# A two-layer decoder on one core: more pairs by seven products, the last norm by token halves, and one constant on another queue

## The chip, the cores and the metric

The kernel runs on one core of one Trainium2 chip. The metric is the device time of one execution in microseconds (us); the median of three runs is given. TensorE (PE; PEld is its weight load), VectorE (DVE), ScalarE (ACT) and the DMA queues of SyncE (SP) and ACT do the work; GpSimd (POOL) only sets up constants.

## What is computed

The reference is a trunk of two layers on 256 tokens of width 2048, in float32. Layer 0 mixes tokens by a causal pooling mixer, layer 1 by differential attention (8 heads, two softmax maps each, subtracted); after each comes a SwiGLU block with inner width 5632; RMS norm ahead of every part and at the end.

```python
for i in range(2):
    hn = rmsnorm(h, norm_mix[i])
    mix = pool_mixer(hn, ...) if i == 0 else diff_attention(hn, ...)
    h = h + mix
    hn = rmsnorm(h, norm_ffn[i])
    h = h + (silu(hn @ w_gate[i]) * (hn @ w_up[i])) @ w_down[i]
return rmsnorm(h, final_norm)
# diff_attention: q, k, v = hn @ w_qkv; a = softmax(q1 k1) - lam * softmax(q2 k2) with ALiBi;
# o = rmsnorm(a @ v, subln_g) * (1 - lambda_init); return o @ w_o
```

## The kernel before

All weight matrices are streamed once, in pieces of 1 MB: a *pair* is 256 rows (two blocks of 128) by 1024 columns (two blocks of 512). `load` brings it (three buffers `raw`, SP's queue), and `halves` splits it into a rounded part `whi` (ACT, line 118) and the remainder `wlo` (DVE, line 119), both in fp32r, since a product in fp32r carries too few bits for one to be enough: each product is made as hi x hi, hi x lo, lo x hi, three TensorE instructions of 128x512 (line 180). The activations (`xp`, `xq`, `h`, `oT`) are held as hi and lo, too, transposed.

`group` makes one product of 256 tokens by 1024 columns over all pairs of a group, in eight PSUM banks `b0` to `b7`. A pair is either *plain*, 8 block products (24 instructions) into the four banks of the result (b4 to b7), or *by seven*, a Strassen-Winograd product: 7 block products (21 instructions) into all of b0 to b6. A pair by seven needs sums of the weight's blocks on DVE (`sums`, lines 124, 126, 127) and their split into `thi` (ACT, 133) and `tlo` (DVE, 134), with one buffer each of tsum, thi and tlo, and an activation operand in eight blocks (`pair` with `seven`, lines 249 to 257, through the buffer `e`) instead of four. Products over different pairs are added up in the banks, so which pairs go by seven is free for each group; the tuples `SEVEN`, `SEVEN_DOWN`, `SEVEN_QK` list them. If a group has a pair by seven, `combined` adds the banks up (two ACT copies, eight DVE operations, lines 190 to 200); if it has none, the banks are the result themselves. Transposes and small products use b0 to b3 (`aux`), too.

The order is: pool mixer (lines 266 to 346), SwiGLU of layer 0 (`ffn`), q and k of four groups of heads, v and attention's output by heads, w_o, SwiGLU of layer 1. In `ffn` the 11 gate/up groups come in chunks of 4, 4 and 3; behind each chunk come two down groups (o = 0, 1), whose pairs are the h tiles of the chunk, 8, 8 and 6. In the first gate/up group of each layer only pair 6 goes by seven, in the others 2, 4 and 6. Down has pairs 2 and 5 by seven, but none in the last group of layer 1. After the last chunk the residual's square sums are made (`square_sum`, line 220), and either the next operand is transposed or, at the end, the row scale is computed for all tokens (`row_scale`), and four `ys` tiles of 512 columns are scaled and stored (lines 402 to 412).

The Tile framework reorders the instructions of each engine when the kernel is built, by priorities and its own cost model; each engine then runs its list in order. So the order in the code is not always that of the trace.

The start: x (2 MB in four DMAs) goes on SP's queue, `band` (the pooling matrices, 768 KB) and the gains on ACT's; two plain pool weights follow on SP, and `scale_in` (1 MB) and `dist` on ACT. Per token half the squares of x give a row scale, band is multiplied by it (line 296), and only then come TensorE's first products (lines 313 to 315).

Of the kernel before, what the change touches and what calls it, by code (L numbers as in the profile page):

```python
# [9 lines left out]
F32 = mybir.dt.float32  # L10
F32R = mybir.dt.float32r
# [5 lines left out]
P = 128  # L17
# [20 lines left out]


SEVEN = (2, 4, 6)  # L40
SEVEN_DOWN = (2, 5)
SEVEN_QK = (4, 6)


B12, B11, B22, B21 = range(4)
# [6 lines left out]
def trunk_kernel(ctx, tc, x_n, gains, scale_in, final_in, subln, lam_in, band, dist,  # L52
# [46 lines left out]
    def operand(seven=()):  # L99

        return [resid.tile(pair_shape(p in seven), F32R, name="xp", tag=f"xp{p}") for p in range(NP)]
# [166 lines left out]
    with tc.tile_pool(name="start", bufs=1, reuse_waits="tile") as st:  # L268
# [8 lines left out]
        for t in range(2):  # L277
            for i in range(2):
                cols = slice(i * 1024, (i + 1) * 1024)
                nc.sync.dma_start(out=x_tok[:, t, cols], in_=x_n[:, t, cols])  # L280
        nc.scalar.dma_start(out=band_sb, in_=band)
        nc.scalar.dma_start(out=gain_sb, in_=gains)
        w_plain = [st.tile([P, 4, 512], F32, name=f"w{g}") for g in range(PLAIN)]
        for g in range(PLAIN):
# [65 lines left out]
    def ffn(layer, xq, ss, next_op, next_gain):  # L350

        ss_next = tmp.tile([P, 2, 4], F32, name="ss")
        r = row_scale(ss)
        with tc.tile_pool(name=f"ffn{layer}", bufs=1, reuse_waits="tile") as hp:
            g0 = 0
            ys = []
            for c, n in enumerate(CHUNKS):
                last = c == len(CHUNKS) - 1
                hp_tiles = []
                if last and next_op is None:  # L360
                    final_sb = [hp.tile([P, 1024], F32, name="final_sb", tag=f"h{6 + i}") for i in range(2)]
                    for i in range(2):
                        nc.scalar.dma_start(out=final_sb[i], in_=final_in[:, i * 1024:(i + 1) * 1024])
                for g in range(g0, g0 + n):

                    by_seven = SEVEN[-1:] if g == 0 else SEVEN
                    cs = combined(group([(xq[p], p in by_seven, w_gu[layer][g, p]) for p in range(NP)], hp), hp)
                    for t in range(2):
                        gate, up = cs[t]
                        nc.scalar.activation(gate, gate, AF.Silu, scale=r[:, t:t + 1])  # L370
                        nc.vector.scalar_tensor_tensor(up, up, r[:, t:t + 1], gate, ALU.mult, ALU.mult)
                    for i in range(2):
                        at = 2 * (g - g0) + i
                        ht = hp.tile(pair_shape(at in SEVEN_DOWN), F32R, name="h", tag=f"h{at}")
                        pair(ht, lambda k, t: cs[t][1][:, (2 * i + k) * P:(2 * i + k + 1) * P], None, at in SEVEN_DOWN)
                        hp_tiles.append(ht)
                for o in range(2):
                    if last and o == 1:

                        pre = tmp.tile([P, 8], F32, name="warm", bufs=1)  # L380
                        nc.scalar.activation(pre[:, 0:1], x_tok[:, 0, 0:1], AF.Square)
                        nc.scalar.activation(pre[:, 0:1], pre[:, 0:1], AF.Sqrt)

                    by_seven = () if last and o and next_op is None else SEVEN_DOWN
                    cs = combined(group([(hp_tiles[i], i in by_seven, w_down[layer][o, 2 * g0 + i])
                                         for i in range(2 * n)], hp), hp)
                    for b in range(2):
                        j = 2 * o + b
                        for t in range(2):
                            cols = slice(j * 512, (j + 1) * 512)  # L390
                            nc.vector.tensor_tensor(x_tok[:, t, cols], cs[t][b], x_tok[:, t, cols], ALU.add)
                            if last:
                                square_sum(ss_next, t, j)
                            if last and next_op is None:
                                if t == 0:
                                    ys.append(hp.tile([P, 2, 512], F32, name="y", tag=("y0", "y1", "h0", "h3")[j]))
                                nc.vector.tensor_tensor(ys[j][:, t], x_tok[:, t, cols],
                                                        final_sb[j // 2][:, j % 2 * 512:j % 2 * 512 + 512], ALU.mult)
                        if last and next_op is not None:
                            transposed(next_op, j, next_gain, SEVEN_QK)  # L400
                g0 += n
            if next_op is None:

                r = row_scale(ss_next)
                for j in range(4):
                    for t in range(2):
                        if t or j > 1:
                            nc.vector.tensor_scalar(ys[j][:, t], ys[j][:, t], r[:, t:t + 1], None, ALU.mult)
                        else:
                            nc.scalar.activation(ys[j][:, t], ys[j][:, t], AF.Copy, scale=r[:, t:t + 1])  # L410
                    (nc.scalar if j % 2 else nc.sync).dma_start(
                        out=out[:, j * 512:(j + 1) * 512].rearrange("(t p) n -> p t n", p=P), in_=ys[j])
        return ss_next

    xp = operand(SEVEN_QK)
    ss = ffn(0, xq, ss, xp, 3)


# [1 line left out]
    with tc.tile_pool(name="attn", bufs=1, reuse_waits="tile") as ap_, ExitStack() as heads:  # L420
# [15 lines left out]
        nc.vector.tensor_scalar(gs, subln_sb, 1.0 - LAMBDA_INIT, None, ALU.mult)  # L436
        aT = []

        def scaled(cs, scales, pool=None):

            out = [[pool.tile([P, 512], F32, name="tok", tag=f"tok{t}{b}", bufs=2) if pool else cs[t][b] for b in range(2)]
                   for t in range(2)]
            for b, scale in enumerate(scales):
                for t in range(2):
                    nc.scalar.activation(out[t][b], cs[t][b], AF.Copy, scale=scale[:, t:t + 1])
            return out

        def transpose_probs(h, probs):

# [39 lines left out]

        for g in range(4):  # L490

            cs = combined(group([(xp[p], p in SEVEN_QK, w_qk[g, p]) for p in range(NP)], hq), hq)
            cs = scaled(cs, (qs_col, r_col))
            for u in range(2):
                qk = at.tile([P, 2, 2, S], F32, name="qk", bufs=3)
                for b in range(2):
                    tp = aux((P, 2, S))
                    for c in range(2):
                        for t in range(2):
                            nc.tensor.transpose(tp[:, c, t * P:(t + 1) * P],  # L500
                                                cs[t][b][:, (2 * u + c) * P:(2 * u + c + 1) * P], ident)
                    nc.scalar.copy(qk[:, b], tp)
                head(2 * g + u, qk)
# [3 lines left out]

        oT = [None] * NP
        for g in range(2):
            cs = scaled(combined(group([(xp[p], False, w_v[g, p]) for p in range(NP)], op_), op_), (r_col, r_col), op_)  # L510
            for h in range(4 * g, 4 * g + 4):
                v = [cs[t][h % 4 // 2][:, h % 2 * E:(h % 2 + 1) * E] for t in range(2)]
                op = aux((P, 2, E))
                nc.tensor.matmul(op[:, 0, :], aT[h][:, 0], v[0], start=True, stop=True)  # L514
                nc.tensor.matmul(op[:, 1, :], aT[h][:, 1], v[0], start=True, stop=False)  # L515
                nc.tensor.matmul(op[:, 1, :], aT[h][:, 2], v[1], start=False, stop=True)  # L516
                oss = at.tile([P, 2], F32, name="o_ss")
                for t in range(2):
                    sq = tmp.tile([P, 512], F32, name="sq", bufs=1)[:, :E]
                    nc.scalar.activation(sq, op[:, t, :], AF.Square, accum_out=oss[:, t:t + 1])  # L520
                ro = rsqrt(oss, E, 2)
                on = at.tile([P, 2, E], F32, name="o_n", bufs=1)
                for t in range(2):
                    nc.scalar.activation(on[:, t, :], op[:, t, :], AF.Copy, scale=ro[:, t:t + 1])
                oT[h] = op_.tile(pair_shape(False), F32R, name=f"oT{h}")
                pair(oT[h], lambda i, t: on[:, t, i * P:(i + 1) * P], [gs[:, i:i + 1] for i in range(2)], False)
        xq = operand(SEVEN)
        for g in range(2):
            cs = combined(group([(oT[p], False, w_o[g, p]) for p in range(NP)], ap_), ap_)
            for b in range(2):  # L530
                j = 2 * g + b
                cols = slice(j * 512, (j + 1) * 512)
                for t in range(2):
                    nc.vector.tensor_tensor(x_tok[:, t, cols], cs[t][b], x_tok[:, t, cols], ALU.add)
                    square_sum(ss_next, t, j)
                transposed(xq, j, 4, SEVEN)
# [85 lines left out]
```

## Time and profile before

| | |
|---|---|
| median of three runs | 1865.94 us (1865.7 to 1866.75) |
| profiled execution | 1866.35 us |
| its span | 1864.6 us |
| PE, PEld, DVE, ACT busy | 1840.9, 1511.5, 1509.8, 1002.0 us |
| granted TensorE clock, mean | 0.998 |
| DMA | 356.74 MB, 191 GB/s over the span |

The span goes from the first to the last instruction that was profiled; a little of the execution lies around it. PE's busy time counts an instruction from its start to its modelled end, and instructions overlap. In groups of instructions a row gives line, engine, operation, result and operands, shapes and count, then the group's busy time, the mean of one in ns, and the idle time ahead of it with what ended it. In the chain each piece has start, length and what ran; in the timeline each row has start, length, engine, line and operation, with the idle time ahead of it and its releaser in brackets.

### The profile page before, as it was taken

The page shows a single profiled execution, that of the slowest core. Times are in us where ns is not written, and L with a number is a line of the kernel's source. Part 1 is how long each engine was busy: PE and PEld are TensorE (multiplying, and loading weights), DVE is VectorE, ACT ScalarE, POOL GpSimd, SP SyncE. Part 2 cuts the span into 40 slices and gives each one's busy share as a digit, 9 for nine tenths or more (in the row PEclk, how much of TensorE's full clock was granted, in tenths as well). Part 3 has the DMA queues.
Part 4 walks back from the last instruction along what each step waited for, and adds up shares of the span by engine and source line. Part 5 has one row for each costly group of instructions (what it writes and reads, how often), then busy time and mean ns, then how long its engine had stood idle before and what let it go on. Part 6 is the DMA issues. An engine that isn't in the chain of part 4 may idle for free.

```text
span 1864.6 us, 20847 instructions
## 1 busy us (share of the span) xinstructions
PE 1840.9 (99%) x8298; PEld 1511.5 (81%) x8298; DVE 1509.8 (81%) x1531; ACT 1002.0 (54%) x965; POOL 0.7 (0%) x6
## 2 busy tenths in 40 slices
PE   8999999999999999999999999999999999999997
PEld 6888888888888887788888888888888888888885
DVE  4789988899888899888864455798888899878885
ACT  5555544555544556656656544555544555445553
POOL 0000000000000000000000000000000000000000
PEclk9999999999999999999999999999999999999999
DMA  6455555555555555555554455555555555665552
GB/s 269 158 203 188 196 203 200 190 208 192 203 203 203 190 194 181 182 182 179 174 173 166 165 180 181 191 208 190 202 203 203 194 190 196 210 226 199 186 202 90
DMA packets 50721, 356.74 MB, mean 191 GB/s; under 512 B 5952, under 2 KB 6080, under 8 KB 8000
## 3 DMA queue, kind: packets, MB, share of 16 engines
q1 hardware_dynamic: 49216, 351.30, 54.5%
q10 hardware_dynamic: 1408, 4.11, 0.6%
q8 instruction: 65, 1.06, 0.2%
q14 instruction: 32, 0.26, 0.0%
HBM read 353.29 MB, written 2.10 MB: 191 GB/s over the span
## 4 chain that ended last, share of the span: by engine, by line
PE 96%; DVE 1%; issue 1%; ACT 1%; DMA 0%; SPq 0%; DVEq 0%; ACTq 0%
PE b L180 91%; PE b L239 2%; PE b L323 1%; PE b L330 1%; PE b L470 1%; DMA x_tok<-x_n 0%; PE b L500 0%; ACT whi L118 0%; PE b L314 0%; PE b L313 0%; DVE wlo L119 0%; PE b L514 0%; PE b L516 0%; PE b L515 0%; PE b L455 0%
## 5 line engine op out<-in xcount | busy, mean ns | idle before, releaser
L119 DVE TENSOR_TENSOR wlo<-raw,whi 128x1536 fp32r<-128x1536 f32 (+1 forms) x330 | 706.0, 2139 | 285.2 <-ACT whi L118 285.0
L118 ACT CAST whi<-raw 128x1536 fp32r<-128x1536 f32 (+1 forms) x330 | 591.9, 1794 | 636.7 <-PE b L180 534.8
L180 PE MATMUL b<-whi,xp 128*128 128x512 f32 x2884 | 926.6, 392 | 1.0 <-DVE c L192 1.0
L180 PEld LDWEIGHTS b<-whi,xp 128*128 128x128 f32 x2884 | 539.7, 188 | 112.5 <-issue 1.4
L180 PE MATMUL b<-wlo,xp 128*128 128x512 f32 x1442 | 562.8, 390 | 0.5 <-DVE wlo L119 0.5
L180 PE MATMUL b<-whi,h 128*128 128x512 f32 x1188 | 377.0, 391 | 2.8 <-DVE c L192 2.1
L180 PEld LDWEIGHTS b<-wlo,xp 128*128 128x128 f32 x1442 | 270.9, 188 | 55.5 <-DVE wlo L119 0.9
L180 PEld LDWEIGHTS b<-whi,h 128*128 128x128 f32 x1188 | 222.5, 188 | 50.6 <-DVE c L197 1.6
L180 PE MATMUL b<-wlo,h 128*128 128x512 f32 x594 | 231.4, 390 | 0.0
L134 DVE TENSOR_TENSOR tlo<-tsum,thi 128x2048 fp32r<-128x2048 f32 x92 | 210.3, 2285 | 7.9 <-ACT thi L133 7.7
L180 PE MATMUL b<-thi,xp 128*128 128x512 f32 x560 | 195.2, 389 | 0.0
L133 ACT CAST thi<-tsum 128x2048 fp32r<-128x2048 f32 x92 | 175.6, 1909 | 13.7 <-DVE tsum L127 13.6
L180 PEld LDWEIGHTS b<-wlo,h 128*128 128x128 f32 x594 | 111.5, 188 | 23.0 <-DVE wlo L119 0.3
L180 PEld LDWEIGHTS b<-thi,xp 128*128 128x128 f32 x560 | 105.1, 188 | 21.7
L124 DVE TENSOR_TENSOR tsum<-raw 128x1024 f32<-128x1024 f32 x92 | 112.3, 1220 | 2.5 <-DMA raw<-w_down 1.1
L180 PE MATMUL b<-tlo,xp 128*128 128x512 f32 x280 | 109.6, 391 | 0.0
L180 PE MATMUL b<-whi,oT 128*128 128x512 f32 x256 | 80.5, 392 | 0.0
L127 DVE TENSOR_TENSOR tsum<-tsum,raw 128x512 f32<-128x512 f32 x92 | 63.3, 689 | 2.0
L126 DVE TENSOR_TENSOR tsum<-tsum,raw 128x512 f32<-128x512 f32 x92 | 63.1, 686 | 0.8
L180 PEld LDWEIGHTS b<-tlo,xp 128*128 128x128 f32 x280 | 52.6, 188 | 13.2 <-DVE tlo L134 2.5
L180 PE MATMUL b<-thi,h 128*128 128x512 f32 x176 | 61.3, 389 | 0.0
L180 PEld LDWEIGHTS b<-whi,oT 128*128 128x128 f32 x256 | 48.2, 188 | 9.8
(130 smaller groups left out, 1114.2 us busy)
## 6 DMA issues: line engine op xcount, KB each, us to landing
raw<-w_gu SPq DMA_DIRECT2D x176, 1024.0 KB, 4.8
raw<-w_down SPq DMA_DIRECT2D x88, 1024.0 KB, 4.9
raw<-w_qk SPq DMA_DIRECT2D x32, 1024.0 KB, 4.8
raw<-w_v SPq DMA_DIRECT2D x16, 1024.0 KB, 4.8
raw<-w_o SPq DMA_DIRECT2D x16, 1024.0 KB, 4.8
x_tok<-x_n SPq DMA_DIRECT2D x4, 512.0 KB, 7.0
w<-pool_w SPq DMA_DIRECT2D x2, 1024.0 KB, 11.9
raw<-pool_w SPq DMA_DIRECT2D x2, 1024.0 KB, 13.2
```

Source lines behind the costliest of these rows:

```text
L118: nc.scalar.copy(hi[:, lo_block:], raw[:, lo_block:])
L119: nc.vector.tensor_tensor(lo[:, lo_block:], raw[:, lo_block:], f32(hi[:, lo_block:]), ALU.subtract)
L124: nc.vector.tensor_tensor(t[:, T1:T3 + 1], raw[:, B11:B22 + 1], raw[:, B12:B12 + 1].broadcast_to([P, 2, 512]), ALU.add)
L126: nc.vector.tensor_tensor(t[:, T2], t[:, T1], raw[:, B22], ALU.add)
L127: nc.vector.tensor_tensor(t[:, T4], t[:, T2], raw[:, B21], ALU.add)
L133: nc.scalar.copy(hi, t)
L134: nc.vector.tensor_tensor(lo, t, f32(hi), ALU.subtract)
L180: nc.tensor.matmul(ps[b], x, y[:, block], start=first, stop=(left[b] == 0))
L239: nc.tensor.transpose(ps[:, i, 1 - t if seven else t], src(i, t), ident)
L323: nc.tensor.matmul(zp[g][t], a[:, t * P:(t + 1) * P], w[:, at], start=(at == 0), stop=(at == 3))
L330: nc.tensor.matmul(zp[g][t], u, y[:, at], start=(at == 0 and j == 0), stop=(at == 3 and j == 2))
L470: nc.tensor.matmul(sc[:, :nk], qk[:, 0, c, qb * P:(qb + 1) * P], qk[:, 1, c, :nk], start=True, stop=True)
```

## The change

- `SEVEN_DOWN` is (2, 4, 6) instead of (2, 5); in a chunk of three groups, with pairs 0 to 5, that is (2, 4).
- The first gate/up group of layer 1 uses pairs 2, 4, 6; that of layer 0 still only 6.
- v uses pairs 4 and 6, w_o pair 6. Their groups are combined; v's scaling by `scaled` is done in place instead of into tiles `tok`; o_n shares the buffer of `e`; head 6's operand is in eight blocks.
- The last down group visits its blocks by token half, and each half's row scale, scaling and two output DMAs stand behind its second block; `ys` is two tiles in the buffers of tsum and thi.
- `band` goes on SP's queue behind x instead of on ACT's.

```diff
-SEVEN_DOWN = (2, 5)
-SEVEN_QK = (4, 6)
+SEVEN_DOWN = (2, 4, 6)
+SEVEN_QKV = (4, 6)
+SEVEN_O = (6,)
...
-        nc.scalar.dma_start(out=band_sb, in_=band)
+        nc.sync.dma_start(out=band_sb, in_=band)
         nc.scalar.dma_start(out=gain_sb, in_=gains)
...
-                    by_seven = SEVEN[-1:] if g == 0 else SEVEN
+                    by_seven = SEVEN[-1:] if g == 0 and layer == 0 else SEVEN
...
-                    for b in range(2):
+                    ends = last and o and next_op is None
+                    for b, t in ((0, 0), (1, 0), (0, 1), (1, 1)) if ends else ((0, 0), (0, 1), (1, 0), (1, 1)):
                         j = 2 * o + b
-                        for t in range(2):
-                            cols = slice(j * 512, (j + 1) * 512)
-                            nc.vector.tensor_tensor(x_tok[:, t, cols], cs[t][b], x_tok[:, t, cols], ALU.add)
-                            if last:
-                                square_sum(ss_next, t, j)
-                            if last and next_op is None:
-                                if t == 0:
-                                    ys.append(hp.tile([P, 2, 512], F32, name="y", tag=("y0", "y1", "h0", "h3")[j]))
-                                nc.vector.tensor_tensor(ys[j][:, t], x_tok[:, t, cols],
-                                                        final_sb[j // 2][:, j % 2 * 512:j % 2 * 512 + 512], ALU.mult)
-                        if last and next_op is not None:
-                            transposed(next_op, j, next_gain, SEVEN_QK)
+                        cols = slice(j * 512, (j + 1) * 512)
+                        nc.vector.tensor_tensor(x_tok[:, t, cols], cs[t][b], x_tok[:, t, cols], ALU.add)
+                        if last:
+                            square_sum(ss_next, t, j)
+                        if last and next_op is None:
+                            if b == 0 and t == 0:
+                                ys.append(hp.tile([P, 2, 2, 512], F32, name="y", tag=("tsum", "thi")[o]))
+                            nc.vector.tensor_tensor(ys[o][:, t, b], x_tok[:, t, cols],
+                                                    final_sb[o][:, b * 512:(b + 1) * 512], ALU.mult)
+                        if last and t and next_op is not None:
+                            transposed(next_op, j, next_gain, SEVEN_QKV)
+                        if ends and b:
+                            tot = tmp.tile([P, 2], F32, name="ss_tot")
+                            nc.vector.tensor_reduce(tot[:, 0:1], ss_next[:, t], AX.X, ALU.add)
+                            rt = rsqrt(tot[:, 0:1], D, 1)
+                            for i in range(2):
+                                nc.scalar.activation(ys[i][:, t, 0], ys[i][:, t, 0], AF.Copy, scale=rt)
+                                nc.vector.tensor_scalar(ys[i][:, t, 1], ys[i][:, t, 1], rt, None, ALU.mult)
+                                (nc.scalar if i else nc.sync).dma_start(
+                                    out=out[t * P:(t + 1) * P, i * 1024:(i + 1) * 1024],
+                                    in_=ys[i][:, t].rearrange("p b n -> p (b n)"))
...
-            if next_op is None:
-                r = row_scale(ss_next)
...
-            cs = scaled(combined(group([(xp[p], False, w_v[g, p]) for p in range(NP)], op_), op_), (r_col, r_col), op_)
+            cs = scaled(combined(group([(xp[p], p in SEVEN_QKV, w_v[g, p]) for p in range(NP)], op_), op_), (r_col, r_col))
...
-                on = at.tile([P, 2, E], F32, name="o_n", bufs=1)
+                on = tmp.tile([P, 2, E], F32, name="o_n", tag="e", bufs=1)
...
-                oT[h] = op_.tile(pair_shape(False), F32R, name=f"oT{h}")
+                oT[h] = op_.tile(pair_shape(h in SEVEN_O), F32R, name=f"oT{h}")
...
-            cs = combined(group([(oT[p], False, w_o[g, p]) for p in range(NP)], ap_), ap_)
+            cs = combined(group([(oT[p], p in SEVEN_O, w_o[g, p]) for p in range(NP)], op_), op_)
```

More of the change, by code (lines that the diff above doesn't have):

```diff
@@ L401, in ffn @@
-                g0 += n
-            if next_op is None:
-                r = row_scale(ss_next)
[L405 to L412, printed above, removed]
+                        cols = slice(j * 512, (j + 1) * 512)
@@ L413, in ffn @@
+                g0 += n
         return ss_next
-    xp = operand(SEVEN_QK)
+    xp = operand(SEVEN_QKV)
     ss = ffn(0, xq, ss, xp, 3)
@@ L437, in trunk_kernel, with scaled @@
         aT = []
-        def scaled(cs, scales, pool=None):
-            out = [[pool.tile([P, 512], F32, name="tok", tag=f"tok{t}{b}", bufs=2) if pool else cs[t][b] for b in range(2)]
-                   for t in range(2)]
+        def scaled(cs, scales):
             for b, scale in enumerate(scales):
                 for t in range(2):
-                    nc.scalar.activation(out[t][b], cs[t][b], AF.Copy, scale=scale[:, t:t + 1])
-            return out
+                    nc.scalar.activation(cs[t][b], cs[t][b], AF.Copy, scale=scale[:, t:t + 1])
+            return cs
         def transpose_probs(h, probs):
@@ L490, in trunk_kernel @@
         for g in range(4):
-            cs = combined(group([(xp[p], p in SEVEN_QK, w_qk[g, p]) for p in range(NP)], hq), hq)
+            cs = combined(group([(xp[p], p in SEVEN_QKV, w_qk[g, p]) for p in range(NP)], hq), hq)
             cs = scaled(cs, (qs_col, r_col))
@@ L521, in trunk_kernel @@
                 ro = rsqrt(oss, E, 2)
-                on = at.tile([P, 2, E], F32, name="o_n", bufs=1)
+                on = tmp.tile([P, 2, E], F32, name="o_n", tag="e", bufs=1)
                 for t in range(2):
                     nc.scalar.activation(on[:, t, :], op[:, t, :], AF.Copy, scale=ro[:, t:t + 1])
-                oT[h] = op_.tile(pair_shape(False), F32R, name=f"oT{h}")
-                pair(oT[h], lambda i, t: on[:, t, i * P:(i + 1) * P], [gs[:, i:i + 1] for i in range(2)], False)
+                oT[h] = op_.tile(pair_shape(h in SEVEN_O), F32R, name=f"oT{h}")
+                pair(oT[h], lambda i, t: on[:, t, i * P:(i + 1) * P], [gs[:, i:i + 1] for i in range(2)], h in SEVEN_O)
         xq = operand(SEVEN)
         for g in range(2):
-            cs = combined(group([(oT[p], False, w_o[g, p]) for p in range(NP)], ap_), ap_)
+            cs = combined(group([(oT[p], p in SEVEN_O, w_o[g, p]) for p in range(NP)], op_), op_)
             for b in range(2):
```

## The prediction

> **What bounds the kernel now.** I read the page first (busy shares and the chain that ended last), then the chain in order of time, then the waits, then the groups of instructions, and last the stretches and the timeline around each place that the change touches.
>
> ```profile
> span 1864.6 us, 20847 instructions
> PE 1840.9 (99%) x8298; PEld 1511.5 (81%) x8298; DVE 1509.8 (81%) x1531; ACT 1002.0 (54%) x965; POOL 0.7 (0%) x6
> PE 96%; DVE 1%; issue 1%; ACT 1%; DMA 0%; SPq 0%; DVEq 0%; ACTq 0%
> ```
> ```profile
> 231.42 125.40 PE b L180 x553
> ```
>
> TensorE is the bound: 99% busy and 96% of the chain. A busy PE could still be a slow PE, so the pace has to be checked: the chain has one unbroken piece of 553 products in 125.40 us, 226.8 ns each. That is the price of one 128x512 product of line 180, with no stall in it. VectorE, at 81%, is next; ACT at 54% has room for everything added below.
>
> The profiled execution took 1866.35 us, 1.8 us more than its span, and lies 0.4 us above the median of 1865.94. The sum below is made against 1866.35, and the 0.4 is taken off at the end. A change under about 0.2% (3.7 us) cannot be told from none here.
>
> **The products saved.** A plain pair costs 4 blocks x 2 parts x 3 = 24 products, a pair by seven 7 x 3 = 21. Pairs that become sevens: down, in the two chunks of 4 groups 3 instead of 2 pairs, for two outputs and two layers: 2 x 2 x 2 = 8 (the chunk of 3 has pairs 0 to 5, so (2, 4) instead of (2, 5): no more than before; the last product of layer 1 stays plain); first gate/up group of layer 1, pairs 2 and 4: 2; v, pairs 4 and 6 in two groups: 4; w_o, pair 6 in two groups: 2. In all 16, so 48 products x 226.8 ns = **-10.9 us**, as long as VectorE delivers in time. Nothing hides these products, so all of it counts.
>
> **What the sevens cost VectorE.**
>
> ```profile
> L119 DVE TENSOR_TENSOR wlo<-raw,whi 128x2048 fp32r<-128x2048 f32 x238 | 544.8, 2289 | 269.5 <-ACT whi L118 269.4
> L134 DVE TENSOR_TENSOR tlo<-tsum,thi 128x2048 fp32r<-128x2048 f32 x92 | 210.3, 2285 | 7.9 <-ACT thi L133 7.7
> L119 DVE TENSOR_TENSOR wlo<-raw,whi 128x1536 fp32r<-128x1536 f32 x92 | 161.2, 1752 | 15.7 <-ACT whi L118 15.6
> L124 DVE TENSOR_TENSOR tsum<-raw 128x1024 f32<-128x1024 f32 x92 | 112.3, 1220 | 2.5 <-DMA raw<-w_down 1.1
> L127 DVE TENSOR_TENSOR tsum<-tsum,raw 128x512 f32<-128x512 f32 x92 | 63.3, 689 | 2.0
> L126 DVE TENSOR_TENSOR tsum<-tsum,raw 128x512 f32<-128x512 f32 x92 | 63.1, 686 | 0.8
> L192 DVE TENSOR_TENSOR c<-b,c 128x512 f32<-128x512 f32 x37 | 25.2, 682 | 0.1
> L244 DVE TENSOR_TENSOR h<-b,h 128x512 fp32r<-128x512 f32 x32 | 21.0, 681 | 0.0
> L257 DVE TENSOR_TENSOR h<-e,h 128x1024 fp32r<-128x1024 f32 x12 | 14.6, 1218 | 0.0
> L253 DVE TENSOR_TENSOR e<-e 128x256 f32<-128x256 f32 x20 | 8.3, 416 | 0.4 <-ACT e L252 0.4
> L255 DVE TENSOR_TENSOR e<-e 128x128 f32<-128x128 f32 x20 | 5.7, 286 | 0.3
> L254 DVE TENSOR_TENSOR e<-e 128x128 f32<-128x128 f32 x20 | 5.6, 282 | 0.1
> ```
>
> A seven adds 1.22 + 0.69 + 0.69 + 2.29 us of sums and remainder and shortens the weights' remainder from 2.29 to 1.75: +4.34 us. An h tile in eight blocks takes 1.22 + 0.42 + 0.28 + 0.29 = 2.20 instead of 0.68: +1.52. A group that has sevens for the first time (v, w_o) adds eight operations of 0.68 to combine, 5.5 us. Whether that is free is seen in the stretches (columns: us, then busy time with the number of instructions for PE, PEld, DVE, ACT, POOL, then clock, DMA share, GB/s).
>
> ```profile
> 146.00:230.00 84.00, 84.00 (x376) 69.05 (x375) 76.57 (x69) 48.30 (x38) 0.00 (x0) 1.00 0.58 197
> 230.00:314.50 84.50, 84.50 (x379) 70.01 (x378) 69.66 (x61) 41.27 (x27) 0.00 (x0) 1.00 0.58 200
> 112.00:366.50 254.50, 254.50 (x1139) 210.19 (x1138) 221.06 (x191) 132.97 (x97) 0.00 (x0) 1.00 0.58 199
> 1143.00:1160.00 17.00, 17.00 (x85) 14.25 (x84) 14.79 (x25) 11.45 (x22) 0.00 (x0) 1.00 0.50 174
> 1160.00:1192.00 32.00, 32.00 (x143) 26.50 (x142) 22.69 (x17) 16.97 (x12) 0.00 (x0) 1.00 0.56 195
> ```
>
> Row 1 is two gate/up groups: three sevens in eight pairs, DVE 91% busy, PE never idle. Row 2 is the two down groups of a chunk, DVE 82%. Row 3 is a whole chunk, 254.5 us, DVE 221.1. With the change a chunk of four gets two sevens and one h tile more: 221.1 + 8.7 + 1.5 = 231.3 us in 254.5 - 1.4 = 253.1, or 91%, what row 1 already sustains. Locally the margin shrinks:
>
> ```profile
> 161.90 2.29 DVE L134 TENSOR_TENSOR tlo<-tsum,thi 128x2048 fp32r<-128x2048 f32 x1
> 165.23 0.39 PE L180 MATMUL b<-tlo,xp 128*128 128x512 f32 x1
> 246.42 2.29 DVE L134 TENSOR_TENSOR tlo<-tsum,thi 128x2048 fp32r<-128x2048 f32 x1 [0.39 <-ACT thi L133]
> 255.56 0.39 PE L180 MATMUL b<-tlo,h 128*128 128x512 f32 x1
> ```
>
> In a gate/up group tlo is done 1.0 us before its first product (161.90 + 2.29 to 165.23), in a down group 6.9 us before. Sevens two pairs apart wait for the single tsum/thi/tlo buffer, so down will run at the margin of 1.0 us. That margin holds in gate/up, where the work beside it is of the same size (combination, then four residual adds here, two products and two h tiles there), so I expect it to hold: **+0.5 us**, bounds 0 and 5 (0.6 us at each of the 8 added sevens).
>
> For v and w_o VectorE is half idle around them; the question is the end of a group, where the values now need a combination before ACT's scaling or the residual add. The nearest row is the q/k groups, which end that way (last of the waits below): 0.35 us per group. Four groups: **+1.0**, bounds 0 and 3. What is queued behind: the next group's first pair needs the banks, but in gate/up the same order costs nothing. o_n moves to the buffer of e; both have one buffer, and only head 6 uses both: nothing, hidden by the pairs of w_o ahead of it.
>
> The first gate/up group of layer 1 is tighter. The last two rows of stretches: DVE 14.8 + 22.7 = 37.5 of 49 us. Added are two sevens (8.7) and the four late combining operations of w_o (2.7): 48.9 us in 49 - 1.4 = 47.6. So 1.3 us too much, with the sums of pair 2 queued among the operand's own conversion: **+1.5**, bounds 0 (the sums run earlier) and 4.3 (one seven's work wholly late). What is saved there in products, 1.4, is then spent.
>
> **Stalls that go.** PE's idle time outside start and end:
>
> ```profile
> PE b L180 <- DVE c L192: 3.1, 3, 1.0
> PE b L180 <- DVE c L197: 0.8, 2, 0.5
> PE b L180 <- DVE wlo L119: 0.5, 1, 0.5
> PEld b L500 <- ACT c L445: 1.4, 4, 0.4
> ```
>
> The first three rows are six waits at three places: behind the down products of the chunk of three, layer 0 (two) and layer 1 (one), where pair 5, the last, is a seven. Its banks end late and the combination begins only then, so the next group waits for its first bank. With (2, 4) the last pair is plain, as in the chunks of four and in gate/up, where the list has no such wait. 3.1 + 0.8 + 0.5 = 4.4 us; I take **-4.0**. Late next is the same combination's last operation, some tenths.
>
> **Start.** The DMAs are at 396 to 428 GB/s there, so the order of the bytes decides.
>
> ```profile
> 11.06 1.06 ACT L291 ACTIVATE sq_in<-x_tok 128x1024 f32<-128x1024 f32 x1 [0.69 <-DMA x_tok<-x_n]
> 11.18 0.75 DVE L296 TENSOR_SCALAR band_sb<-band_sb,rs_r 128x1024 f32<-128x1024 f32 x1
> 11.98 1.78 PEld L313 LDWEIGHTS b<-band_sb,x_tok 128*128 128x128 f32 x8 [6.59 <-DVE band_sb L296]
> scale_sb<-scale_in ACTq DMA_DIRECT2D x1, 1024.0 KB, 9.4
> ```
> ```profile
> 3.00:6.00 3.00, 2.69 (x13) 2.39 (x12) 0.00 (x0) 0.00 (x0) 0.00 (x0) 1.00 0.99 396
> 10.00:14.00 4.00, 2.02 (x8) 1.78 (x8) 2.71 (x12) 1.72 (x6) 0.00 (x0) 1.00 1.01 428
> ```
>
> The last piece of x is in at 11.06 now, band having gone before; in the new order band is the last of the same bytes, in at 10.2 to 11.0. x comes earlier by band's 0.79 MB (2 us), so the first row scale is there at about 9.2 (11.18 less 2), and the scaling of band (0.75) starts at 10.2 to 11.0, not 11.18. PE starts 0.2 to 1.0 us earlier: **-0.6**. SP issues one DMA more ahead of the pool weights, 0.4 us that their queue hides: they come after x and band as before. Lower bound -1.5; the upper, +1.4, is a rival below.
>
> **End.**
>
> ```profile
> 1852.35 0.39 PE L180 MATMUL b<-whi,h 128*128 128x512 f32 x1
> 1855.88 0.17 DVE L226 COPY r_tok<-rs_r 128x2 f32<-128x2 f32 x1
> 1856.09 2.46 DVE L408 TENSOR_SCALAR y<-y,r_tok 128x512 f32<-128x512 f32 x6
> 1857.45 1.53 ACTq L411 DMA_DIRECT2D out_t<-y  x2
> out_t<-y ACTq DMA_DIRECT2D x2, 512.0 KB, 4.5
> ```
>
> From the last product's end (1852.74) to the span's end are 11.9 us: 3.3 to the row scale, 2.5 of scaling, 0.4 of issue, 4.5 of landing, 1.1 behind it. Afterwards the first token half is normalised during the last products and its 1 MB leaves first. The second half still needs add, square, sum and root: 3.3, plus about 0.4 for ACT's scaling of the first half ahead of it; two scalings of 0.67 on ACT, DVE beside it: 1.3; issue 0.4; landing 3.6 to 4.5, say 3.9, with fewer bytes ahead; 1.1 behind: 10.4. So **-1.5**, bounds 0 and -2.6.
>
> **Sum.** -10.9 - 4.0 - 0.6 - 1.5 + 0.5 + 1.0 + 1.5 = -14.0: 1866.35 - 14.0 = 1852.35, and 0.4 off for the median: **1851.9 us**.
>
> **Rivals.**
>
> *The joints cost more* (v, w_o, the first group of layer 1 at their upper bounds, 7.3 instead of 2.5, and half of the stalls that should go staying, +2): 1851.9 + 6.8 = 1858.7. For it: DVE is over-booked in that first group. Against: the half-idle DVE at v and w_o.
>
> *Band comes later, not earlier.* scale_in (1.05 MB) stays on ACT's queue, where band was ahead of it. If it takes turns with band on SP's queue, band comes after 4.0 MB at 0.40 MB/us from 2 us on, at about 12.6; PE starts at 13.4 instead of 11.98: 1851.9 + 0.6 + 1.4 = 1853.9. Against it: before, scale_in needed 9.4 us from issue to landing, as if it had waited for x, and not taken turns. [...]
>
> *The halves bring nothing at the end* (ACT's scalings of the first half stand ahead of the second half's squares): 1851.9 + 1.5 = 1853.4.
>
> *VectorE becomes the bound in down*, the slower side: the added work of the 8 down sevens and 4 h tiles, 8 x 4.34 + 4 x 1.52 = 40.8 us, falls on PE. At full price 1851.9 - 0.5 + 40.8 = 1892.2; it makes the kernel no faster from 14.5 of the 40.8, a third. For it: the margin of 1.0 us. Against: 91% in gate/up without an idle PE.
>
> **How the numbers follow.** Forecast 0.60; joints 0.17; band 0.10; end 0.08; VectorE in down 0.05. The time is that of the forecast. Its own range is 1848 to 1855.5 (bounds of stalls and end); band and end lie in it; the range reaches to the joints: 1846.8 (all gains at their bounds, new stalls halved) to 1858.0. Faster by over 0.2% means below 1862.2: all cases but the last, less a little for several bounds at once, 0.94; the last is split, same 0.03, slower 0.03.
>
> **What would show it.** 108 sums of the first kind instead of 92 and 48 fewer products of line 180; pieces of the chain of 553 products again at 226.8 ns; no PE wait for the combination behind the chunk of three; DVE at about 91% in down with PE unbroken; PE's first product of band at about 11.4 us; 10.4 us from last product to span's end. Wrong would be: new PE waits for tlo or wlo in down, over 1 us in the first gate/up group of layer 1, or band in after 12 us.

## The result, and the profile after

The changed kernel takes 1856.06 us (median of 6 runs, 1855.69 to 1856.82), the kernel before 1865.95 (6 runs beside them, 1865.56 to 1866.78): a ratio of 0.9947, 95% interval 0.9937 to 0.9957, or -9.9 us. The forecast was -14.0 and a time of 1851.9; the time lies in the forecast's range of 1846.8 to 1858.0. The profiled execution took 1855.69 us, its span 10.9 us shorter than before. The sum is compared with these 10.9.

The page: span, busy shares, the chain's shares and the group of first sums.

```profile
span 1853.7 us, 20951 instructions
PE 1831.7 (99%) x8250; PEld 1500.6 (81%) x8250; DVE 1594.9 (86%) x1644; ACT 1035.7 (56%) x1001; POOL 0.7 (0%) x6
PE 93%; DVE 3%; DMA 1%; ACT 1%; issue 1%; SPq 0%; ACTq 0%; DVEq 0%
L125 DVE TENSOR_TENSOR tsum<-raw 128x1024 f32<-128x1024 f32 x108 | 131.8, 1220 | 3.6 <-DMA raw<-w_v 1.4
```

48 PE instructions fewer and 108 first sums instead of 92, as the change says. PE is still the bound. But its share of the chain fell from 96% to 93% and DVE's rose from 1% to 3%: the chain now runs through VectorE at more places. (After's lines are numbered one higher than before's up to the tail of the attention.)

The waits of PE and of its weight loads over the whole span (us in total, times, longest), then the stretch of one whole chunk of four:

```profile
PE b L314 <- DVE band_sb L297: 8.8, 1, 8.8
PE b L181 <- DVE c L193: 0.7, 1, 0.7
PE b L181 <- DVE c L198: 0.4, 1, 0.4
PEld b L181 <- DVE tlo L135: 6.8, 17, 0.4
```
```profile
112.00:365.00 253.00, 253.00 (x1129) 208.35 (x1128) 228.83 (x202) 136.48 (x100) 0.00 (x0) 1.00 0.57 199
```

Row 1 was 6.3: PE's first product of band came later, not earlier. Rows 2 and 3 were 3.1 and 0.8: the stalls behind the chunk of three went, and what is left stands elsewhere. Row 4 was 2.5 us in 6 waits: eleven new waits for tlo. The stretch has DVE at 228.8 of 253, 90%, where 91% were forecast.

Where the 10.9 us come from, by the starts of the weight groups in the two traces:

| stretch | after - before, us | forecast |
|---|---|---|
| up to the third gate/up group of layer 0 (+0.9 at the first) | +0.7 | -0.6 |
| the four chunks of four | -0.76, -0.75, -0.79, -0.80 = -3.1 | -5.4 products, +0.5 |
| the chunk of three and the group behind it (layers 0, 1) | -3.4, -1.6 = -5.0 | -4.0 |
| v to the third gate/up group of layer 1 | -2.1 | -5.4 products, +2.5 |
| behind the last product | -1.6 | -1.5 |

The "-5.4 products" are 24 x 226.8 ns each. The other groups add 0.1 us together.

### The profile page after: what moved, and what is told of

The parts are those of the page before. It is cut to its first block, busy times and chain, and to the rows that moved or that the text cites. A ratio compares the mean times of both kernels' runs of the same rounds, so it can differ in the third digit from the quotient of the medians.

```text
span 1853.7 us, 20951 instructions
## 1 busy us (share of the span) xinstructions
PE 1831.7 (99%) x8250; PEld 1500.6 (81%) x8250; DVE 1594.9 (86%) x1644; ACT 1035.7 (56%) x1001; POOL 0.7 (0%) x6
## 3 DMA queue, kind: packets, MB, share of 16 engines
q8 instruction: 64, 1.05, 0.2%
## 4 chain that ended last, share of the span: by engine, by line
PE 93%; DVE 3%; DMA 1%; ACT 1%; issue 1%; SPq 0%; ACTq 0%; DVEq 0%
PE b L181 88%; PE b L240 2%; DVE wlo L120 1%; PE b L324 1%; PE b L331 1%; PE b L469 1%; DMA band_sb<-band 1%; PE b L499 0%; ACT whi L119 0%; DMA raw<-w_down 0%; PE b L314 0%; DMA raw<-w_v 0%; DVE tsum L125 0%; DMA raw<-w_gu 0%; PE b L315 0%
## 5 line engine op out<-in xcount | busy, mean ns | idle before, releaser
L181 PE MATMUL b<-whi,xp 128*128 128x512 f32 x2824 | 908.7, 392 | 0.9 <-DVE c L193 0.7
L181 PE MATMUL b<-whi,h 128*128 128x512 f32 x1108 | 354.8, 390 | 0.4 <-DVE c L198 0.4
L135 DVE TENSOR_TENSOR tlo<-tsum,thi 128x2048 fp32r<-128x2048 f32 x108 | 246.7, 2285 | 3.9 <-ACT thi L134 3.9
L181 PE MATMUL b<-wlo,h 128*128 128x512 f32 x554 | 215.8, 390 | 0.0
L134 ACT CAST thi<-tsum 128x2048 fp32r<-128x2048 f32 x108 | 206.2, 1909 | 14.4 <-DVE tsum L128 14.3
L181 PE MATMUL b<-thi,xp 128*128 128x512 f32 x608 | 211.8, 390 | 0.0
L125 DVE TENSOR_TENSOR tsum<-raw 128x1024 f32<-128x1024 f32 x108 | 131.8, 1220 | 3.6 <-DMA raw<-w_v 1.4
L181 PEld LDWEIGHTS b<-wlo,h 128*128 128x128 f32 x554 | 104.0, 188 | 21.3
L181 PE MATMUL b<-thi,h 128*128 128x512 f32 x240 | 83.7, 389 | 0.0
L128 DVE TENSOR_TENSOR tsum<-tsum,raw 128x512 f32<-128x512 f32 x108 | 74.4, 689 | 2.2
L127 DVE TENSOR_TENSOR tsum<-tsum,raw 128x512 f32<-128x512 f32 x108 | 74.0, 685 | 0.7
L181 PEld LDWEIGHTS b<-thi,h 128*128 128x128 f32 x240 | 45.1, 188 | 9.2
## 6 DMA issues: line engine op xcount, KB each, us to landing
raw<-pool_w SPq DMA_DIRECT2D x2, 1024.0 KB, 13.4
```

The costliest lines, as they stand in the source:

```text
L125: nc.vector.tensor_tensor(t[:, T1:T3 + 1], raw[:, B11:B22 + 1], raw[:, B12:B12 + 1].broadcast_to([P, 2, 512]), ALU.add)
L127: nc.vector.tensor_tensor(t[:, T2], t[:, T1], raw[:, B22], ALU.add)
L128: nc.vector.tensor_tensor(t[:, T4], t[:, T2], raw[:, B21], ALU.add)
L134: nc.scalar.copy(hi, t)
L135: nc.vector.tensor_tensor(lo, t, f32(hi), ALU.subtract)
L181: nc.tensor.matmul(ps[b], x, y[:, block], start=first, stop=(left[b] == 0))
```

## The experiments

Each kernel is the changed one with one edit. "After" is the changed kernel's trace; ratios are to the kernel before.

**The start: why band is late.** The issues and the first scaling in after's timeline (start, us, engine, line, operation):

```profile
0.73 0.41 ACTq L283 DMA_DIRECT2D gain_sb<-gains  x1
1.24 0.39 ACTq L299 DMA_DIRECT2D scale_sb<-scale_in  x1
2.77 0.58 SPq L282 DMA_DIRECT2D band_sb<-band  x1
11.25 1.06 ACT L292 ACTIVATE sq_in<-x_tok 128x1024 f32<-128x1024 f32 x1 [0.17 <-DMA x_tok<-x_n]
13.02 0.75 DVE L297 TENSOR_SCALAR band_sb<-band_sb,rs_r 128x1024 f32<-128x1024 f32 x1 [0.24 <-DMA band_sb<-band]
```

and the same DMA in before's timeline:

```profile
6.25 0.33 ACTq L298 DMA_DIRECT2D scale_sb<-scale_in  x1
```

On ACT's queue stood band, gains, then the first square (which waits for x, 6.24 in before) and scale_in. With band gone everything moves up one place: scale_in is out ahead of the square, issued at 1.24 instead of 6.25, and its 1 MB moves beside x. Bytes by queue from 5 to 8 us of after (q10 is ACT's, q1 SP's; packets, MB, share of 16 engines):

```profile
q10 hardware_dynamic: 111, 0.84, 65.8%
q1 hardware_dynamic: 118, 0.42, 34.1%
```

x got one third of the bytes, its last piece came at 11.25 instead of 11.06, and band behind it landed at 13.0. The trace has this order of events; two runs undo it in two ways.

```
e1_band_act:  - nc.sync.dma_start(out=band_sb, in_=band)
              + nc.scalar.dma_start(out=band_sb, in_=band)
e2_scale_sp:  - nc.scalar.dma_start(out=scale_sb, in_=scale_in)     # behind the row scales
              + nc.sync.dma_start(out=scale_sb, in_=scale_in)       # behind the plain pool weights
```

> The changed kernel with band back on ACT's queue, nothing else. Theory (taking turns): band landed at 13.0 us because scale_in, now alone on ACT's queue, shared the DMA engines with x; with band ahead of it again, PE's first band product is at 12.0 us instead of 13.8 and the first gate/up group begins 0.7 to 0.9 us earlier: about 1855.3. Rival (band's place is without effect, the later start comes from the new order of instructions): PE's first product stays at 13.8 and the time at 1856.1.

1854.44 us (1853.46 to 1855.19), ratio 0.9935 (0.992 to 0.995). Scale_in is issued at 6.29 again, PE's first product of band is at 12.03, and gate/up starts 0.7 us earlier than in after. The first product is the firm sign: in after and the six other kernels whose start has the same code it comes at 13.7 to 13.9 us, while their gate/up starts are themselves 1.2 us apart (the last section says why). In the medians this kernel is 1.6 us faster than after.

> The changed kernel with band behind x on SP's queue and scale_in on SP's queue too, behind the two plain pool weights. Theory (taking turns): with nothing large on ACT's queue band lands at about 10.2 us, PE's first band product is at 11.1, and the first gate/up group begins 2 to 2.7 us earlier than in the changed kernel: about 1853.7. Rival (band behind 2 MB of x is late whatever shares the engines): band still lands after 12 us, 1856.1.

1852.13 us (1852.02 to 1852.63), ratio 0.9924 (0.9909 to 0.9938). The first scaling and product of its timeline:

```profile
11.32 1.14 DVE L299 TENSOR_SCALAR band_sb<-band_sb,rs_r 128x1024 f32<-128x1024 f32 x2
12.12 0.80 PE L314 MATMUL b<-band_sb,x_tok 128*128 128x128 f32 x2 [6.43 <-DVE band_sb L299]
```

Band is in at 10.4, as the prediction had wanted it; but VectorE's order sets both scalings behind the second row scale, so PE starts at 12.12, 1.7 us before after. Yet gate/up starts 3.3 us earlier. The other half is the clock. Stretches of e2_scale_sp and then of after (PEclk is the third column from the right):

```profile
8.00:12.00 4.00, 0.00 (x0) 0.00 (x0) 2.03 (x11) 2.17 (x5) 0.00 (x0) 0.69 1.03 434
12.00:16.00 4.00, 3.88 (x17) 3.89 (x18) 0.46 (x2) 0.84 (x2) 0.00 (x0) 0.50 1.01 426
16.00:20.00 4.00, 4.00 (x14) 1.92 (x14) 0.00 (x0) 0.00 (x0) 0.00 (x0) 0.96 1.01 426
20.00:24.00 4.00, 4.00 (x20) 2.56 (x19) 0.00 (x1) 2.63 (x3) 0.00 (x0) 1.00 1.01 428
```
```profile
4.00:8.00 4.00, 1.04 (x8) 0.85 (x7) 0.00 (x0) 1.26 (x3) 0.00 (x0) 0.95 1.02 423
12.00:16.00 4.00, 2.17 (x9) 1.92 (x9) 2.10 (x8) 0.60 (x3) 0.00 (x0) 0.50 1.03 434
16.00:20.00 4.00, 4.00 (x15) 3.25 (x15) 0.00 (x0) 0.84 (x2) 0.00 (x0) 0.50 1.01 428
20.00:24.00 4.00, 4.00 (x13) 2.00 (x12) 0.00 (x0) 0.09 (x1) 0.00 (x0) 0.84 1.01 428
```

Worked out of these shares, half clock is granted from about 9.5 to 16.3 us in the one and from 7.6 to 21.3 in the other. At half clock stand 4.2 us of products (12.1 to 16.3) against 7.5 (13.8 to 21.3); the difference of 3.3, at half speed, costs 1.65. With the 1.7 of the earlier start that is 3.35, the 3.3 measured. In e1 the clock came at 21.5: 1.8 us earlier at work, 9.5 us at half clock, so 1.8 - 1.0 = 0.8 gained, 0.7 measured. So two things set the start, band behind scale_in and the time at which the full clock comes; the last section goes into the second.

**Layer 1's first group and w_o.** The weight loads' waits in that group in after (products of pairs 4 and 6, then the next group's first bank):

```profile
1167.17 0.76 PEld L181 LDWEIGHTS b<-thi,xp 128*128 128x128 f32 x4 [0.28 <-ACT thi L134]
1177.75 0.76 PEld L181 LDWEIGHTS b<-thi,xp 128*128 128x128 f32 x4 [0.42 <-ACT thi L134]
1185.13 0.19 PEld L181 LDWEIGHTS b<-whi,xp 128*128 128x128 f32 x1 [1.17 <-DVE c L193]
```

The sevens run one behind the other and late, and the combination later still.

```
e3_g0_six:    by_seven = SEVEN[-1:] if g == 0 else SEVEN                      # pair 6 alone in both layers
e4_wo_plain:  group([(oT[p], False, w_o[g, p]) for p in range(NP)], op_)      # w_o plain
```

> The changed kernel with only pair 6 by seven in the first gate/up group of layer 1, as before the change. Theory (VectorE is over-booked there): 6 products more, 1.4 us, but the waits in and behind that group, 2.2 us over the pace, go; from the group's start to that of the third gate/up group 0.8 us less, 1855.3. Rival (the waits come from w_o's new combination ahead of it): they stay, and the time is 1.4 us more, 1857.5.

1855.15 us (1854.3 to 1855.96), ratio 0.9938 (0.9921 to 0.9954). From the group's start to the third group it is 0.72 us shorter than after, with six products more: the two sevens together cost 2.1 us where their products save 1.4. In its profile the gain is used up elsewhere, at places that the edit does not touch: it reaches the group 0.7 us later than after (0.4 of it from the start; up to the second q/k group it loses another 0.7 and then wins 0.3 back), and behind the last product it takes 0.6 us longer.

> The changed kernel with w_o's groups plain: no combination behind them, 6 products more. If w_o's sevens pay in full: 1.4 us longer over w_o, 1857.4. If the combination of w_o is what over-books VectorE in the first gate/up group of layer 1 (5.5 us of DVE), that group's waits of 2.2 us fall by at least 1 us, and the time is 1856.0 to 1856.5.

1855.02 us (1853.96 to 1855.29), ratio 0.9937 (0.9923 to 0.9952). From w_o's first group to the third gate/up group it is 0.50 us shorter than after, again with six products more; of the group's waits one of 0.36 us is left. So w_o's sevens do not pay ahead of that group as it is: theirs and its work together are too much for that stretch.

**v.**

```
e10_vo_plain:  group([(xp[p], False, w_v[g, p]) for p in range(NP)], op_)     # v plain, w_o plain
```

> The changed kernel with v and w_o both plain. Against the version with w_o plain alone (1855.0) it shows v by itself: 12 products, 2.7 us, if their combination is hidden, so 1857.7; if v's combination costs PE 0.35 us per group as in the q/k groups, 1857.0; if it eats the gain, 1855.0.

1855.87 us (1855.54 to 1856.9), ratio 0.9944 (0.993 to 0.9959). From v's first group to the third gate/up group: before 284.05 us, this kernel 283.01, the one with w_o alone plain 281.44. The first group's two sevens by themselves bring 1.0 of their 1.36 us; v's four bring 1.6 of 2.7, nearest to the second of the three cases. (The whole times are 0.85 us apart in the medians and 1.97 in the two profiles; the stretch leaves out what differs elsewhere.)

**Down.** The rows of weight loads that wait in the first chunk, from the waits by kernel (before had 0.4, 1): after, then (2, 4), then (2, 5).

```
e6_down_24:  SEVEN_DOWN = (2, 4)
e7_down_25:  SEVEN_DOWN = (2, 5)
```
```profile
PEld b L181 <- DVE tlo L135: 1.3, 3, 0.4
```
```profile
PEld b L181 <- DVE tlo L135: 0.8, 2, 0.4
```
```profile
PEld b L181 <- DVE tlo L135: 0.4, 1, 0.4
```

> The changed kernel with pairs (2, 4) by seven in every down group: no third seven in the chunks of four, the chunk of three as in the changed kernel. The 8 sevens cost 24 products back, 5.4 us; the first traces give only 0.77 us per chunk for them. If the waits for tlo (0.27 us in the group before and 0.27 in the first down group) come from the third seven, each of the four chunks is 0.8 us longer and the time is 1859.2; if those waits are there for another reason and stay, 1.36 us longer each, 1861.5.

1858.69 us (1857.71 to 1859.48), ratio 0.9958 (0.9943 to 0.9973). A chunk of four takes 1.07 to 1.14 us longer than after; the chunk of three is the same within 0.1 in layer 1, and in layer 0 it is 0.7 shorter. That stretch of layer 0 scatters: in the nine other traces that have after's code there, four of them (e3, e4, e8, e10) with the very same order of instructions up to its end, it takes 236.7 to 238.7 us (after 237.3, before 240.7). What makes the scatter was not found.

> The changed kernel with the old pairs (2, 5) in every down group. The number of products is that of (2, 4). Theory (a seven as the last pair makes the combination late): in the chunk of three the waits come back, 3.4 us in layer 0 and 1.6 in layer 1, so 5.0 us more than with (2, 4), 1864.2; the chunks of four, where pair 5 isn't the last, are as with (2, 4). Rival (those gains came from another place, such as the new order of instructions around): within 1 us of (2, 4).

1862.85 us (1862.16 to 1863.57), ratio 0.9981 (0.9972 to 0.9991). As many products as with (2, 4), and 4.2 us slower. The chunk of three with what follows it costs 3.4 more than after in layer 0 and 1.6 in layer 1, 5.0 together, and its waits of PE are those of before again:

```profile
PE b L181 <- DVE c L193: 3.9, 4, 1.0
PE b L181 <- DVE c L198: 0.8, 2, 0.5
PE b L181 <- DVE wlo L120: 0.5, 1, 0.5
```

So the stalls were the last pair's seven. (With the scatter of layer 0 their worth there is 2.1 to 4.1 us, of which after's trace shows 3.4; in layer 1 it is 1.2 to 1.7.) In the chunks of four (2, 5) is only 0.8 us slower than after, and 0.3 faster than (2, 4): each step, from (2, 5) to (2, 4) to (2, 4, 6), adds one wait of the rows above, which costs about 0.3 us. Two places are new in after: pair 2 of the chunk's last gate/up group (199.04 us) and pair 2 of the first down group (241.79). The third sevens themselves bring 1.1 of 1.36.

The wait could be for the single buffer of thi and tlo, or for the engines:

```
e9_thi2:  hi = pool.tile([P, 4, 512], F32R, name="thi", bufs=TB if pool.name.startswith("ffn") else 1)   # TB = 2; tlo's line is as before
```

To make room, dist's tile and its load lie in the attention's part, one unused gain is left out, the squares that are thrown away are bf16, and the second `ys` tile lies in tlo's buffer.

> The changed kernel with two buffers of thi and of tlo in the SwiGLU blocks (room made by dist in the attention's pool, the unused sixth gain left out, and the squares' throw-away result in bf16). Theory (the single buffer holds tlo back): the waits of 0.27 us in the last gate/up and the first down group of each chunk go, 0.5 us per chunk, 2 us in all: 1854.0. Rival (VectorE comes late with tsum itself, whatever the buffers): the waits stay, 1856.1.

1855.67 us (1855.13 to 1856.14), ratio 0.9943 (0.993 to 0.9957). The row of the first chunk:

```profile
PEld b L181 <- DVE tlo L135: 1.2, 3, 0.4
```

All three waits are there. But the edit gives a second buffer to thi alone; tlo keeps its single one, though the expectation names both. So the run rules out thi's buffer and says nothing of tlo's. After's own trace does, at the third place:

```profile
236.11 2.29 DVE L120 TENSOR_TENSOR wlo<-raw,whi 128x2048 fp32r<-128x2048 f32 x1 [0.68 <-ACT whi L119]
238.32 1.22 DVE L258 TENSOR_TENSOR h<-e,h 128x1024 fp32r<-128x1024 f32 x1
239.45 2.28 DVE L135 TENSOR_TENSOR tlo<-tsum,thi 128x2048 fp32r<-128x2048 f32 x1
```

VectorE goes without a pause from the remainder of h tile 6, new in eight blocks, to tlo, whose thi was done at 238.83. So tlo waits for its turn on VectorE and not for a buffer. The same holds at every place of the kind: in before, after, (2, 4) and (2, 5) alike, each wait of 0.4 us stands 14.3 us behind the start of a group that follows an h tile 2, 4 or 6 in eight blocks. With (2, 5) there is one such place in a chunk of four, with (2, 4) two, with (2, 4, 6) three; tile 5, the second of its group, has its remainder behind tlo and costs no wait. So what makes tlo late is the longer h tile ahead of it in VectorE's list, not the seven itself: in (2, 4) the first down group has a seven at pair 2, too, with a tile 6 in four blocks, and no wait. An order with tlo ahead of that remainder was not tried.

**The end.**

```
e8_end_all:  - for b, t in ((0, 0), (1, 0), (0, 1), (1, 1)) if ends else ((0, 0), (0, 1), (1, 0), (1, 1)):
             + for b, t in ((0, 0), (0, 1), (1, 0), (1, 1)):
             -     if ends and b:          # row scale, scalings and outputs of token half t
             + if next_op is None:         # behind the last block: one row scale, then the same
             +     r = row_scale(ss_next)
```

> The changed kernel with one row scale for all tokens behind the last block, and the four scalings and outputs behind it; blocks visited by columns. Theory (the first half's outputs and norm lie beside the last products): 1.6 us more from the last product to the span's end, 10.3 to 11.9, 1857.7. Rival (the gain came from the smaller last transfers alone, which this version has, too): within 0.5 us of 1856.1.

1856.73 us (1856.24 to 1857.97), ratio 0.9949 (0.9934 to 0.9964). The whole time cannot tell it from after; the tail can. From the last product's end to the span's end: before 11.83 us, this kernel 11.70, after 10.27. After's first half is on its way before the second half's row scale is known:

```profile
1843.01 0.39 PE L181 MATMUL b<-whi,h 128*128 128x512 f32 x1
1845.49 1.32 ACT L408 ACTIVATE y<-y,rs_r 128x512 f32<-128x512 f32 x2
1846.84 0.35 ACTq L410 DMA_DIRECT2D out_t<-y  x1
1847.24 1.33 ACT L408 ACTIVATE y<-y,rs_r 128x512 f32<-128x512 f32 x2 [0.43 <-DVE rs_r L215]
1848.60 0.35 ACTq L410 DMA_DIRECT2D out_t<-y  x1
```

So in these two traces 1.43 of the 1.56 us is the split by halves. The tail scatters, too: in the ten other traces with after's code there it takes 10.27 to 10.90 us, so the split is worth 0.8 to 1.43. This kernel's profile is 1.1 us longer elsewhere too: 2 us at the entry to q/k, against 0.5 won at the start and 0.7 in the down group before, none of which the edit touches; the order of instructions there is the same as in after.

**Versions put together from these.**

```
best_a:  e2_scale_sp and e3_g0_six
best_b:  e2_scale_sp, and that group: (SEVEN[-1:] if layer == 0 else SEVEN[1:]) if g == 0 else SEVEN   # pairs 4, 6
best_c:  best_a, and SEVEN_QKV = (2, 4, 6)
```

> scale_in on SP's queue behind the pool weights, and only pair 6 by seven in the first gate/up group of layer 1; the rest as in the changed kernel. If the two gains add up (about 2.9 and 0.7): 1852.1 - 0.7 = 1851.4. If w_o's combination and not the sevens behind it is what the group waits for: 1.4 more than with scale_in alone, 1853.5.

1852.18 us (1851.65 to 1852.52), ratio 0.9924 (0.9911 to 0.9938). No faster than e2 alone, though that group is 0.7 us shorter here too: its profile loses 0.45 us ahead of the last down groups and 0.3 behind the last product.

> scale_in on SP's queue behind the pool weights, and pairs 4 and 6 by seven in the first gate/up group of layer 1. If it is the seven at pair 2, due while the operand is still converted, that makes VectorE late, pair 4 pays in full: 0.7 us less than with pair 6 alone, 1850.7. If VectorE is short over the whole group: no gain against pair 6 alone, 1851.4 or more.

1851.29 us (1851.13 to 1851.51), ratio 0.992 (0.9906 to 0.9933), the fastest of all. The stretch of layer 1's first two groups is 1.4 us shorter than in after with three products more, and in place of the waits shown above stands only this:

```profile
1182.51 0.19 PEld L181 LDWEIGHTS b<-whi,xp 128*128 128x128 f32 x1 [0.17 <-DVE c L198]
```

Pair 4 by seven pays in full; it was pair 2, right behind the operand's own conversion, that did not, with w_o's combination ahead of it.

> scale_in on SP's queue, only pair 6 in the first gate/up group of layer 1, and in q, k and v pairs 2, 4 and 6 by seven: 6 sevens more, 18 products, 4.1 us. VectorE is 82 to 88% busy in q and k and half idle in v. If it holds as in gate/up: 1851.4 - 4.1 = 1847.3. If the heads' work between makes tlo late: 0.3 us per added seven, 1849.1. If VectorE is the bound in q and k: no gain, 1851.4.

1861.03 us (1859.87 to 1862.08), ratio 0.9971 (0.996 to 0.9982). 18 products fewer than best_a, worth 4.1 us, and 8.9 us slower. From q/k's first group to v's it takes 2.9 us more than best_a, from there to the third gate/up group 4.6 more. Its waits of PE in the window from 700 to 1200 us, where after has 0.7 us on weight products:

```profile
PE b L181 <- ACT thi L134: 2.6, 2, 1.8
PE b L181 <- DVE c L198: 1.7, 3, 0.7
PE b L181 <- DVE tlo L135: 1.5, 1, 1.5
```

These are the blocks with the heads' own work on VectorE and ScalarE; a third seven is late there. The rows name 5.8 us of the about 11.6 lost; the rest is in shorter waits and in the products' order, and was not split further.

## Why the prediction was right or wrong

**Right: what counts.** The chain's longest piece in after:

```profile
232.45 124.36 PE b L181 x547
```

TensorE is the bound and its pace stayed: 227.3 ns for each of 547 products, with one of the new waits (241.79, 0.3 us) inside. So 48 products fewer are worth what they cost wherever the values arrive in time. The rival in which VectorE becomes the bound in down did not come. The three signs of being wrong that the prediction names did come, though: new waits for tlo in down, more than 1 us in layer 1's first group, and band in after 12 us. The time lies in the range because these are small beside the products.

**Right: the stalls.** -4.0 forecast, -5.0 measured, and e7 puts back 5.0. The rows of waits gave 4.4, of which 4.0 were taken. With the scatter of those stretches the stalls are worth 3.2 to 5.7 us, so the difference to the forecast is not shown to be more than that.

**Right: the end.** -1.5 forecast, -1.57 measured, 10.27 us against 10.4, and e8 gives 1.43 of it back; with the scatter of the tail (10.27 to 10.90) it is 0.9 to 1.57, so the close hit is in part luck. The first half is not "normalised during the last products" either: its scaling starts at 1845.49, 2.1 us behind the last product's end, and what is won is that its bytes leave ahead of the second half's.

**Wrong: the start, -0.6 forecast, +0.7 measured.** The step that failed: "In the new order band is the last of the same bytes, in at 10.2 to 11.0", with x 2 us earlier. It took scale_in to stay where it was in time, but taking band off ACT's queue let scale_in out before the square that had held it to 6.25 us. The rival "band comes later" had the event and its size: it gave a start at 13.4 and 1.4 us later than before, and PE started at 13.83. It was held unlikely because 9.4 us from issue to landing were read as "it waited for x"; but that DMA was issued at 6.25, half-way through x, and one time from issue to landing cannot tell waiting from sharing. (By its own figures, 4.0 MB at 0.40 MB/us from 2 us on, that rival's band would be in at 12.0 and not 12.6; the trace has 13.0.) The shares of q10 and q1 above are the direct row: from 5 to 8 us of after 111 and 118 packets came from the two queues, nearly one for one, so scale_in moved beside x and did not wait for it.

Even with band in at 10.4, as in e2, PE did not start at the forecast's time, since VectorE's order put both scalings behind the second row scale.

Of the 1.85 us that PE came later than before (13.83 against 11.98), 0.9 arrived at gate/up. Before's clock column shows full clock there, but its products do not run at it; two lines of its timeline, each early and late:

```profile
14.77 0.45 PE L315 MATMUL b<-band_sb,x_tok 128*128 128x16 f32 x2
22.89 0.29 PE L315 MATMUL b<-band_sb,x_tok 128*128 128x16 f32 x2
18.18 4.86 PE L323 MATMUL b<-w,mean 128*128 128x512 f32 x8
24.00 3.60 PE L323 MATMUL b<-w,mean 128*128 128x512 f32 x8
```

One by one, the products of the third row start 0.85 us apart until 20.7 us and 0.43 behind it, and 20.7 is also where that trace has its first record of the clock. So before worked at the slow pace from 11.98 to 20.7, 8.7 us, and after for 7.5. The 1.2 us less, at half speed, make up 0.6 of the 1.85; of the other 1.2 us 0.9 arrived, and 0.3 stays open.

**Wrong in size: down, +0.5 forecast, +2.3 measured.** "That margin holds in gate/up" was the step. The margin of 1.0 us was read at pair 4 of a gate/up group; at pair 2, behind a first h tile in eight blocks, it did not hold in before either. This row of before's waits is six such places:

```profile
PEld b L180 <- DVE tlo L134: 2.5, 6, 0.4
```

The prediction priced the longer h tile, +1.52 us, in VectorE's total and not in the time ahead of tlo, where it is more than the margin. So tlo is about 0.3 us late in the chunk's last gate/up group and in the first down group, and after's rows of waits show it at just these. Four chunks at -0.77 instead of -1.36 make 2.3. It lies within the bounds given, 0 to 5.

**Wrong in size: v, w_o and the first group, +2.5 forecast, +3.3 measured.** Both terms were of the right sign, and the over-booking of 1.3 us in the first group was real (e3: two sevens cost 2.1 and save 1.4; VectorE is busy for 42.1 of the group's 44.5 us). What the prediction didn't see is that the two terms are one: with w_o plain the waits of the group behind it are nearly gone. Adding up terms for neighbouring groups on one busy engine counts its slack twice. Besides, four groups at the prediction's 0.35 us are 1.4, where it put 1.0.

All terms: start +1.3, down +1.8, joints +0.8, stalls -1.0, end -0.1, together +2.8 of the 3.1 us between -14.0 and -10.9. In the medians the miss is 4.1 us: the profiled execution of before lies 0.4 us above its median and that of after 0.4 below, and after has 0.2 us more outside its span.

## What to carry to other kernels

When a DMA is taken off a queue, look at what moves up behind it: here a 1 MB load came out from behind a compute wait, ran beside the loads that the start hangs on, and turned a gain of some tenths into a loss. Work added to an engine at 90% (VectorE here) was free or not by place, not by average: look at what will stand directly ahead of the value that the bound engine waits for next (here the longer h tile ahead of tlo, about 0.3 us at each place), keep it out of a block's last pair (5.0 us in e7), and price neighbouring groups together. Compare a gain of some tenths with how far traces of the same code lie apart in that stretch (here up to 2 us). And before asking for more of the same saving (best_c), look whether the next block has the same room on the second-busiest engine.

## What the runs showed of the hardware that was not expected

The clock at the start. TensorE began at about half its later pace: in before and after the first products of the warm-up (128x128, from 1.05 us on) start 0.21 us apart; in after they go on 0.11 us apart from 4.2 us, where the trace has its first record of the clock, full. Ahead of that first record the clock column shows full clock, too, so there only the pace tells: in before all twenty start at the slow pace, the last at 5.26 us, and the first record is at 20.7. Full clock lasted 3.4 us in after (TensorE was idle from 5.0 on), then half was granted again, well past the first product of band: 4.2 us of work at half clock in e2, 7.5 in after, 9.5 in e1. That grant of half clock lasted 6.8 us in e2 (9.5 to 16.3) and 13.7 in after (7.6 to 21.3) and in e1 (7.8 to 21.5). It was worth 1.65 us between e2 and after, as much as the loads were. It also accounts for the scatter of 1.2 us in the start among the kernels whose start is the same code as after's (48.4 to 49.65 us to the first gate/up group): in all seven the group starts 31.70 to 31.73 us behind the middle between PE's first product of band and the return of full clock (19.5 to 22.2 us).

A busy PE did not bring full clock here: from 16 to 20 us PE was busy for all 4.00 us in after and in e1, and 0.50 was granted throughout. In e2 full clock came 0.6 us behind the start of the first product of 128x512 (15.69), in after 2.7 us behind it (18.58) and in e1 3.6 us behind it (17.86). What decides when it comes no run shows.
